# A scaled copy at the DMA's pace: five token tiles cut to 26, 25, 26, 25, 26, and the later weights loaded as 16 rows a tile and dealt out by TensorE

## The chip, the core and the metric

The kernel runs on one core of a Trainium2 chip. The metric is the device time of one launch in microseconds; the shorter the better. Beside the time of each run there is a profile of one execution, whose span counts from the first to the last recorded instruction. TensorE, VectorE (DVE), ScalarE (ACT) and GpSimd (POOL) each run their own stream of instructions; SyncE (SP) issues most of the DMA transfers, and sixteen DMA engines carry them.

## The reference

The kernel is the dispatch half of a mixture of experts, without the routing: every token's row is written out once for each of its two experts, scaled by that expert's weight. The indices of the experts are not used.

```python
batch, seq, hidden, n_experts = 16, 1024, 512, 8
k = 2
# x: (16, 1024, 512) f32, expert_weights: (16, 1024, 2) f32
x_expanded = x[:, :, np.newaxis, :].repeat(k, axis=2)
weights = expert_weights[..., np.newaxis]
return (x_expanded * weights).astype(np.float32)
```

So 33.6 MB of x and 131 KB of weights are read, and 67.1 MB are written, with one multiplication for each number written.

## The kernel before

The 16,384 tokens are spread over 128 partitions, 128 tokens to a partition. "Token" below means one such slot: 128 tokens at once, one in each partition, 2 KB of x and 4 KB of output in each. They are cut into five tiles (`groups`), 25, 25, 25, 25 and 28 tokens. Within a tile a partition's tokens lie together in memory, so a load or a store is one long contiguous piece for each partition.

Three buffers fill most of the on-chip memory: `x_pair`, two buffers for x, one for the even tiles and one for the odd ones; `o_ring`, one output buffer of 25 tokens (`TX`); and `w_tile`, all weights, two for each token in each partition. The output buffer is worked in two halves, tokens 0 to 12 (`CUT` = 13) and the rest. In each half VectorE multiplies the first 8 tokens (9 in the first tile) in operations of four tokens (`vector`, through `product`, L97), and ScalarE the others, one expert's row at a time (`scalar`, L120). Then the half is stored.

All transfers but one go through `move` (L65), which issues them from SP in the order in which the program names them. SP is one queue: an issue that waits holds all behind it. The one other transfer, the first tile's weights, is issued by ScalarE. SP's order is:

- the first tile's x in two loads, 9 and 16 tokens (`STEPS`), then all of tile 1's x;
- when the products of tile 0 have been made, tile 2's x, 21 and then 4 tokens, into the buffer that tile 0 leaves, and the weights of tiles 1 to 4, one transfer each (`weights`, L85), 50 or 56 floats to each of 128 partitions;
- tile 0's two stores. The first is held (`wait`, L69) until the load of 21 tokens has landed, so that a stretch of reading from memory ends before a stretch of writing begins;
- tile 1's two stores, then tile 3's x, then tile 4's x in 24 and 4 tokens, and behind it tile 2's two stores, again held until the larger of the two loads has landed;
- tile 3's two stores and tile 4's two stores of 13 and 12 tokens;
- the last tile has 28 tokens and the output buffer 25, so its last three are multiplied into the front of the buffer once the store of that half has landed, and go out as a third piece (L159 to L162).

Of the kernel before, what the change touches and what calls it, by code (L numbers as in the profile page):

```python
# [1 line left out]

# [4 lines left out]


@with_exitstack
def kernel(  # L10
    ctx: ExitStack,
    tc: tile.TileContext,
    x: bass.AP,
    expert_indices: bass.AP,
    expert_weights: bass.AP,
    out: bass.AP,
):
    nc = tc.nc

    batch, seq, hidden = x.shape  # L20
    k = expert_weights.shape[-1]
    P = nc.NUM_PARTITIONS
    ntok = batch * seq
    assert ntok % P == 0
    A_TOTAL = ntok // P

    f32 = mybir.dt.float32
    row = k * hidden
    CH = 4


    groups = [25, 25, 25, 25, 28]
    TX = 25
    CUT = 13
    STEPS = {0: [9, 16], 2: [21, 4], 4: [24, 4]}
    assert sum(groups) == A_TOTAL

    xf = x.rearrange("b s h -> (b s) h")
    of = out.rearrange("b s k h -> (b s) (k h)")
    wf = expert_weights.rearrange("b s k -> (b s) k")  # L40

    w_pool = ctx.enter_context(tc.tile_pool(name="w_pool", bufs=1))
    x_pool = ctx.enter_context(tc.tile_pool(name="x_pool", bufs=1))
    o_pool = ctx.enter_context(tc.tile_pool(name="o_pool", bufs=1))

    w_tile = w_pool.tile([P, A_TOTAL * k], f32)
    o_ring = o_pool.tile([P, TX * row], f32)
    x_pair = [
        x_pool.tile([P, max(groups[e::2]) * hidden], f32, name=f"x{e}")
        for e in range(2)  # L50
    ]

    def rows(of_all, done, T):
        return of_all[done * P : (done + T) * P, :].rearrange(
            "(p a) n -> p (a n)", a=T
        )

    tiles = []
    done = 0
    for n in groups:  # L60
        tiles.append((done, n))
        done += n


    def move(out, in_):  # L65
        return tc.keep_in_program_order(nc.sync.dma_start(out=out, in_=in_))  # L66


    def wait(ins, done):  # L69
        tc.add_manual_dep(  # L70
            ins.ins,
            done.ins.name,
            mybir.DependencyInfo(
                mybir.DependencyClass.Sync, mybir.DependencyReason.DATA
            ),
            reason="turn",
        )

    def load(i, e):
        at = sum(STEPS.get(i, groups[i : i + 1])[:e])  # L80
        to = at + STEPS.get(i, groups[i : i + 1])[e]
        part = slice(at * hidden, to * hidden)
        return move(x_pair[i % 2][:, part], rows(xf, *tiles[i])[:, part])

    def weights(g, to):  # L85
        at, n = tiles[g]
        w = w_tile[:, at * k : (at + (to - g) * n) * k]
        return (
            w.rearrange("p (g m) -> p g m", g=to - g),
            wf[at * P : (at + (to - g) * n) * P, :].rearrange(  # L90
                "(g p a) n -> p g (a n)", g=to - g, p=P
            ),
        )

    def product(o_tile, t, x_in, c, m):
        o = t * row
        nc.vector.tensor_tensor(  # L97
            out=o_tile[:, o : o + m * row].rearrange(
                "p (t k h) -> p t k h", t=m, k=k
            ),  # L100
            in0=x_in[:, : m * hidden]
            .rearrange("p (t h) -> p t h", t=m)
            .unsqueeze(2)
            .to_broadcast([P, m, k, hidden]),
            in1=w_tile[:, c : c + m * k]
            .rearrange("p (t k) -> p t k", t=m)
            .unsqueeze(3)
            .to_broadcast([P, m, k, hidden]),
            op=mybir.AluOpType.mult,
        )  # L110


    def vector(src, c, at, to):
        for t in range(at, to, CH):
            u = min(t + CH, to)
            product(o_ring, t, src[:, t * hidden : u * hidden], c + t * k, u - t)

    def scalar(src, c, at, to):
        return [
            nc.scalar.mul(  # L120
                out=o_ring[:, e * hidden : (e + 1) * hidden],
                in_=src[:, e // k * hidden : (e // k + 1) * hidden],
                mul=w_tile[:, c + e : c + e + 1],
            )
            for e in range(at * k, to * k)
        ]

    def store(dst, at, to):
        return move(dst[:, at * row : to * row], o_ring[:, at * row : to * row])


    out_w, in_w = weights(0, 1)
    nc.scalar.dma_start(out=out_w, in_=in_w)
    load(0, 0)
    load(0, 1)
    load(1, 0)
    for i, (done, n) in enumerate(tiles):
        src, dst, c = x_pair[i % 2], rows(of, done, n), done * k
        v = 9 if i == 0 else 8
        held = i in (0, 2)  # L140
        for at, to in [(0, CUT), (CUT, TX)]:
            vector(src, c, at, at + v)
            scalar(src, c, at + v, to)
            if not held:
                store(dst, at, to)
        if held:
            if i == 0:
                last = load(2, 0)
                load(2, 1)
                for g in range(1, len(tiles)):  # L150
                    move(*weights(g, g + 1))
            else:
                last = load(4, 0)
                load(4, 1)
            for at, to in [(0, CUT), (CUT, TX)]:
                wait(store(dst, at, to), last)
        elif i == 1:
            load(3, 0)
        if n > TX:  # L159
            m = n - TX  # L160
            product(o_ring, 0, src[:, TX * hidden :], c + TX * k, m)
            move(dst[:, TX * row :], o_ring[:, : m * row])  # L162

# [1 line left out]
_INS = ['x', 'expert_indices', 'expert_weights']  # L165
_OUTS = [((16, 1024, 2, 512), 'float32')]


# [23 lines left out]
```

## Time and profile before

| | |
|---|---|
| median of 3 runs | 238.79 us (238.78 to 238.80) |
| the profiled execution | 238.92 us |
| its span | 237.1 us |
| VectorE, ScalarE, GpSimd busy | 93.1, 54.9, 0.2 us |
| SP's DMA queue, share of sixteen engines' span | 98.7% |
| read and written | 33.69 and 67.11 MB |

The page of the profile gives busy times for each engine, the span in forty slices (a digit is tenths, 9 is 90% or more), the DMA queues with the time their packets took, a chain of waits followed back from the last instruction, and groups of instructions by line with their mean duration and with what ended the idle time before them. The timeline lists instructions by start and length in microseconds; for a DMA the issuing instruction stands there, and the time to its landing in the list of issues. TensorE does no work in this kernel.

### The profile page before, as it was taken

The page shows a single profiled execution, that of the slowest core. Times are in us where ns is not written, and L with a number is a line of the kernel's source. Part 1 is how long each engine was busy: PE and PEld are TensorE (multiplying, and loading weights), DVE is VectorE, ACT ScalarE, POOL GpSimd, SP SyncE. Part 2 cuts the span into 40 slices and gives each one's busy share as a digit, 9 for nine tenths or more (in the row PEclk, how much of TensorE's full clock was granted, in tenths as well). Part 3 has the DMA queues.
Part 4 walks back from the last instruction along what each step waited for, and adds up shares of the span by engine and source line. Part 5 has one row for each costly group of instructions (what it writes and reads, how often), then busy time and mean ns, then how long its engine had stood idle before and what let it go on. Part 6 is the DMA issues. An engine that isn't in the chain of part 4 may idle for free.

```text
span 237.1 us, 217 instructions
## 1 busy us (share of the span) xinstructions
DVE 93.1 (39%) x23; ACT 54.9 (23%) x87; POOL 0.2 (0%) x4
## 2 busy tenths in 40 slices
DVE  0499800000094580954900000039195292861300
ACT  0008800000090520914400000037080270800000
POOL 0000000000000000000000000000000000000000
DMA  7999989899999999999999999999999999999996
GB/s 260 474 445 475 423 370 464 372 486 431 420 398 497 464 431 420 398 398 409 475 478 406 398 453 431 431 409 457 484 431 431 409 398 434 449 449 456 423 398 265
DMA packets 3457, 100.80 MB, mean 425 GB/s; under 512 B 1024, under 2 KB 1024, under 8 KB 1024
## 3 DMA queue, kind: packets, MB, share of 16 engines
q1 hardware_dynamic: 3312, 100.77, 98.7%
q10 hardware_dynamic: 144, 0.03, 0.1%
q14 instruction: 1, 0.01, 0.0%
HBM read 33.69 MB, written 67.11 MB: 425 GB/s over the span
## 4 chain that ended last, share of the span: by engine, by line
DMA 70%; DVE 16%; ACT 4%; issue 3%; SPq 0%; DVEq 0%; ACTq 0%
DMA out_dram<-o_ring 46%; DMA x<-in_x_dram 24%; DVE o_ring L97 16%; ACT o_ring L120 3%; ACT L120 1%; SPq L66 0%; DVEq L97 0%; ACTq L120 0%
## 5 line engine op out<-in xcount | busy, mean ns | idle before, releaser
L97 DVE TENSOR_TENSOR o_ring<-x,w_tile 128x4096 f32<-128x4096 f32 (+2 forms) x23 | 93.1, 4096 | 128.5 <-DMA out_dram<-o_ring 105.6
L120 ACT ACTIVATE o_ring<-x,w_tile 128x512 f32<-128x512 f32 x86 | 53.7, 709 | 134.0 <-DMA out_dram<-o_ring 123.3
L120 ACT ACT_TABLE_LOAD x1 | 1.3, 1283 | 18.6 <-DMA x<-in_x_dram 18.6
L176 POOL MEMSET const-bfloat16-1.0<- 128x1 bf16 x1 | 0.1, 102 | 0.0
L176 POOL MEMSET const-uint8-127<- 128x1 uint8 x1 | 0.1, 102 | 0.0
L176 POOL MEMSET const-float32-0.0<- 128x1 f32 x1 | 0.1, 99 | 0.2 <-issue 0.2
L176 POOL MEMSET const-float32-1.0<- 128x1 f32 x1 | 0.1, 99 | 0.0
## 6 DMA issues: line engine op xcount, KB each, us to landing
out_dram<-o_ring SPq DMA_DIRECT2D x5, 6656.0 KB, 21.3
out_dram<-o_ring SPq DMA_DIRECT2D x5, 6144.0 KB, 21.6
x<-in_x_dram SPq DMA_DIRECT2D x2, 6400.0 KB, 34.1
x<-in_x_dram SPq DMA_DIRECT2D x1, 6144.0 KB, 20.6
x<-in_x_dram SPq DMA_DIRECT2D x1, 5376.0 KB, 18.8
x<-in_x_dram SPq DMA_DIRECT2D x1, 4096.0 KB, 17.4
x<-in_x_dram SPq DMA_DIRECT2D x1, 2304.0 KB, 8.1
x<-in_x_dram SPq DMA_DIRECT2D x2, 1024.0 KB, 21.4
```

Of the source, the lines that this page charges most:

```text
L97: nc.vector.tensor_tensor(out=o_tile[:, o : o + m * row].rearrange("p (t k h) -> p t k h", t=m, k=k), in0=x_in[:, : m * hidden] .rearrange ...
L120: nc.scalar.mul(out=o_ring[:, e * hidden : (e + 1) * hidden], in_=src[:, e // k * hidden : (e // k + 1) * hidden], mul=w_tile[:, c + e : c ...
L176: nc = _bacc.Bacc("TRN2", target_bir_lowering=False, num_devices=1)
```

## The change

The tiles become 26, 25, 26, 25 and 26 tokens, and the output buffer 26. Every tile is then stored in two pieces, 13 and 13 or 13 and 12, and the code for the third piece goes. The loads in two steps become 9 and 17, 21 and 5, 22 and 4.

The weights of tiles 1 to 4 are no longer loaded into `w_tile` from behind tile 2's x. They are loaded between the two loads of the first tile, each as 16 rows of 8 x 50 or 8 x 52 floats into 16 partitions, into the part of `o_ring` that the second half of tile 0 will fill later (`room`). Such a row holds what belongs to eight neighbouring partitions. `deal` spreads it: GpSimd makes an identity matrix in `room`; for each tile TensorE transposes eight blocks of 16 rows into a tile in PSUM, ScalarE copies that to `room` with the order of the columns changed, TensorE transposes it back as a whole into one PSUM tile for all four, and ScalarE copies this to `w_tile`. `deal` stands in the program behind the products of the first half of tile 0; in the built program ScalarE's five copies stand ahead of all its multiplications, and the first operation of VectorE's second half waits for the rows, TensorE and GpSimd.

```diff
-    groups = [25, 25, 25, 25, 28]
-    TX = 25
+    groups = [26, 25, 26, 25, 26]
+    TX = max(groups)
     CUT = 13
-    STEPS = {0: [9, 16], 2: [21, 4], 4: [24, 4]}
+    STEPS = {0: [9, 17], 2: [21, 5], 4: [22, 4]}
...
-    def weights(g, to):
...
+    R = 16
+    Q = P // R
+    room = o_ring[:, CUT * row :]
+    eye = room[:, :P]
+    dealt = tiles[1:]
+    skip = dealt[0][0] * k
+    raw = [
+        room[:R, P + (at * k - skip) * Q : P + ((at + n) * k - skip) * Q]
+        for at, n in dealt
+    ]
+    turned = room[:, P + (A_TOTAL * k - skip) * Q :]
+
+    def deal():
+        nc.gpsimd.memset(eye, 1.0)
+        nc.gpsimd.affine_select(
+            out=eye,
+            in_=eye,
+            pattern=[[-1, P]],
+            compare_op=mybir.AluOpType.is_equal,
+            fill=0.0,
+            base=0,
+            channel_multiplier=1,
+        )
+        back = ps_pool.tile([P, A_TOTAL * k - skip], f32)
+        for g, (at, n) in enumerate(dealt):
+            m = n * k
+            mid = ps_pool.tile([m, P], f32, name=f"mid{g}")
+            flat = turned[:m, g * P : (g + 1) * P]
+            for q in range(Q):
+                nc.tensor.transpose(
+                    mid[:, q * R : (q + 1) * R],
+                    raw[g][:, q * m : (q + 1) * m],
+                    eye[:R, :R],
+                )
+            nc.scalar.copy(
+                out=flat.rearrange("m (r q) -> m q r", q=Q),
+                in_=mid.rearrange("m (q r) -> m q r", q=Q),
+            )
+            c = at * k - skip
+            nc.tensor.transpose(back[:, c : c + m], flat, eye[:m, :m])
+        nc.scalar.copy(out=w_tile[:, skip:], in_=back)
...
-    out_w, in_w = weights(0, 1)
-    nc.scalar.dma_start(out=out_w, in_=in_w)
+    nc.scalar.dma_start(out=w_tile[:, :skip], in_=rows(wf, *tiles[0]))
     load(0, 0)
+    for to, (at, n) in zip(raw, dealt):
+        move(
+            to,
+            wf[at * P : (at + n) * P, :].rearrange("(r m) n -> r (m n)", r=R),
+        )
     load(0, 1)
     load(1, 0)
...
-        for at, to in [(0, CUT), (CUT, TX)]:
+        for at, to in [(0, CUT), (CUT, n)]:
             vector(src, c, at, at + v)
             scalar(src, c, at + v, to)
+            if i == 0 and at == 0:
+                deal()
...
                 last = load(2, 0)
                 load(2, 1)
-                for g in range(1, len(tiles)):
-                    move(*weights(g, g + 1))
...
-        if n > TX:
-            m = n - TX
-            product(o_ring, 0, src[:, TX * hidden :], c + TX * k, m)
-            move(dst[:, TX * row :], o_ring[:, : m * row])
```

More of the change, by code (lines that the diff above doesn't have):

```diff
@@ L83, in load @@
         return move(x_pair[i % 2][:, part], rows(xf, *tiles[i])[:, part])
-    def weights(g, to):
[L86 to L92, printed above, removed]
-        )
+    R = 16
[19 more added lines that the diff above has]
+            channel_multiplier=1,
+        )
+        back = ps_pool.tile([P, A_TOTAL * k - skip], f32)
[16 more added lines that the diff above has]
+        nc.scalar.copy(out=w_tile[:, skip:], in_=back)
     def product(o_tile, t, x_in, c, m):
@@ L154 @@
                 load(4, 1)
-            for at, to in [(0, CUT), (CUT, TX)]:
+            for at, to in [(0, CUT), (CUT, n)]:
                 wait(store(dst, at, to), last)
```

2 lines of the change are left out of this document (added).

## The prediction

> **What bounds the kernel now.** I read the page first (engines, the forty slices, the queues), then the chain of waits, then the timeline for the starts of single pieces. The page:
>
> ```profile
> span 237.1 us, 217 instructions
> DVE 93.1 (39%) x23; ACT 54.9 (23%) x87; POOL 0.2 (0%) x4
> ...
> DMA  7999989899999999999999999999999999999996
> ...
> q1 hardware_dynamic: 3312, 100.77, 98.7%
> q10 hardware_dynamic: 144, 0.03, 0.1%
> q14 instruction: 1, 0.01, 0.0%
> HBM read 33.69 MB, written 67.11 MB: 425 GB/s over the span
> ```
>
> VectorE works 39% of the span and ScalarE 23%, while SP's queue q1 fills 98.7% of what the sixteen DMA engines have: 234.0 of 237.1 us. Only the first and last slices fall to 7 and 6 tenths. So the end moves only if q1 gets more or less to do, or if it runs dry somewhere. The bytes of x and of the output are fixed, and both kernels move them once.
>
> The pace comes from the timeline of VectorE in the last third. Each of these starts follows the landing of one stored piece:
>
> ```profile
> 157.85 8.76 DVE L97 TENSOR_TENSOR o_ring<-x,w_tile 128x4096 f32<-128x4096 f32 x2 [39.07 <-DMA out_dram<-o_ring]
> 172.39 8.76 DVE L97 TENSOR_TENSOR o_ring<-x,w_tile 128x4096 f32<-128x4096 f32 x2 [5.77 <-DMA out_dram<-o_ring]
> 188.08 8.76 DVE L97 TENSOR_TENSOR o_ring<-x,w_tile 128x4096 f32<-128x4096 f32 x2 [6.93 <-issue]
> 202.57 8.76 DVE L97 TENSOR_TENSOR o_ring<-x,w_tile 128x4096 f32<-128x4096 f32 x2 [5.73 <-DMA out_dram<-o_ring]
> 218.29 3.36 DVE L97 TENSOR_TENSOR o_ring<-x,w_tile 128x3072 f32<-128x3072 f32 x1 [6.97 <-DMA out_dram<-o_ring]
> ```
>
> From 157.85 to 218.29 are 60.44 us, in which pieces of 12, 13, 12 and 13 tokens landed: 50 tokens of 128 x 4096 B, 26.21 MB, so 433.7 GB/s, or 1.209 us for a stored token and 0.604 us for a loaded one. At this pace the 100.77 MB of q1 take 232.4 us; the 4.7 us left of the span are the start, the end and small items. That is the whole room there is.
>
> The chain of waits shows where q1 might run dry. Its columns are start, length and what:
>
> ```profile
> 1.16 17.37 DMA x<-in_x_dram
> ...
> 27.64 18.75 DMA x<-in_x_dram
> 46.39 0.02 issue
> 46.41 18.56 DMA out_dram<-o_ring
> ...
> 139.52 18.14 DMA out_dram<-o_ring
> ...
> 188.08 8.77 DVE o_ring L97 x2
> 196.85 0.02 SPq L66
> 196.87 0.03 issue
> 196.90 21.27 DMA out_dram<-o_ring
> ```
>
> At 139.52 the first store of tile 2 is issued behind the 4 tokens of the second load of tile 4. It lands 18.14 us later, and 4 loaded plus 13 stored tokens at the pace above are 2.42 + 15.72 = 18.13 us. So 2.42 us of queued work are enough to cover the time from an issue to its first bytes: nothing is lost there. I use 2.42 us below as a cover that suffices.
>
> **The change part by part.**
>
> *The four weight transfers leave the middle.* At 46.41 the first store of tile 0 is issued behind the same 4 loaded tokens and also the four weight transfers, and takes 18.56 us for the same 13 tokens. So the four cost 18.56 - 18.14 = 0.42 us of q1. Their bytes, 204 floats for each of 128 partitions, 104,448 B, are 0.24 us at the pace above; the rest is the price of small pieces. Removed: -0.42 us.
>
> ```profile
> 29.16 1.90 SPq L66 DMA_DIRECT2D w_tile<-in_expert_weights_dram  x4
> ...
> w_tile<-in_expert_weights_dram SPq DMA_DIRECT2D x3, 25.0 KB, 19.7
> w_tile<-in_expert_weights_dram SPq DMA_DIRECT2D x1, 28.0 KB, 19.1
> ```
>
> They had also served as cover for the store at 46.41. Without them 2.42 us would be left; with the fifth token that moves from the first to the second load of tile 2 it is 5 x 0.604 = 3.02 us. Both are at or above the 2.42 us that suffice: 0.
>
> *The same bytes come back between the first tile's two loads*, as four transfers of 16 rows of 1,600 or 1,664 B. Sixteen long pieces in place of 128 short ones speak for less than 0.42 us; that all of them are written into 16 partitions speaks for more. No row of this trace shows such a transfer. Below: their bytes at the full pace, 0.24 us, and not less unless the start hides them (the first slice is at 7 tenths), then 0. Above: if the pace follows the number of partitions written, 16 of 128, it is 54.2 GB/s and 1.93 us. The nearest row is that of the same four transfers with nearly the same bytes, so I take their 0.42 us, and keep 0 and 1.93 as ends. Their issue takes SP 1.90 us by the row above, now ahead of the second load, which would go out near 3.0 us in place of 1.1. It is covered by the first load:
>
> ```profile
> 9.01 19.70 DVE L97 TENSOR_TENSOR o_ring<-x,w_tile 128x4096 f32<-128x4096 f32 x6 [9.01 <-DMA w_tile<-in_expert_weights_dram]
> 18.60 1.28 ACT L120 ACT_TABLE_LOAD   x1 [18.60 <-DMA x<-in_x_dram]
> 19.90 8.68 ACT L120 ACTIVATE o_ring<-x,w_tile 128x512 f32<-128x512 f32 x14
> ```
>
> ```profile
> L97 DVE TENSOR_TENSOR o_ring<-x,w_tile 128x4096 f32<-128x4096 f32 x20 | 87.6, 4421 | 121.5 <-DMA out_dram<-o_ring 98.7 <-issue 13.9 <-DMA w_tile<-in_expert_weights_dram 9.0
> L97 DVE TENSOR_TENSOR o_ring<-x,w_tile 128x1024 f32<-128x1024 f32 x2 | 2.4, 1217 | 0.0
> ```
>
> VectorE starts at 9.01, when the first nine tokens and the weights of tile 0 are there, so q1 is busy nearly until then: 0. The two groups below it are VectorE's operations of four tokens and of one.
>
> [...]
>
> *The first tile's order.* Its second load carries 17 tokens in place of 16. It lands at 18.53 now (1.16 + 17.37), then at 18.53 + 0.60 + 0.42 = 19.55. VectorE has its first nine tokens done at about 19.1 (two operations of 4.42 us and one of 1.22 from 9.01), so it waits some 0.4 us for the second half. The first load of tile 2 needs two operations more and goes out at 19.55 + 8.84 = 28.4 in place of 27.64. q1 then still holds the rest of tile 1: its 25 tokens end 25 x 0.604 = 15.1 us after 19.55, at 34.7. That leaves 6.3 us of cover where 2.42 suffice: 0, with 3.9 us to spare.
>
> *Dealing out.* TensorE makes 32 small transposes and 4 wide ones, ScalarE four copies of 50 or 52 partitions x 128 and one of 128 x 204, GpSimd a memset and a select on 128 x 128. The rows land near 9.5 us. ScalarE's five copies stand ahead of its multiplications, which wait for the second load anyway; its table load moves into the same idle stretch. VectorE's second half writes over the scratch, so it waits for the last transpose. All this has from 9.5 to 19.55, 10 us, and then 3.9 us until q1 runs dry. Five copies at the price of the 128x512 multiplication, 709 ns, are 3.5 us:
>
> ```profile
> L120 ACT ACTIVATE o_ring<-x,w_tile 128x512 f32<-128x512 f32 x86 | 53.7, 709 | 134.0 <-DMA out_dram<-o_ring 123.3
> L176 POOL MEMSET const-uint8-127<- 128x1 uint8 x1 | 0.1, 102 | 0.0
> ```
>
> The transposes have no row; (13.9 - 3.5) / 36 leaves 0.29 us for each, hand-offs included, before anything is late. GpSimd's part is unpriced too, but can start 8 us before the rows are there. I take 0. What is late next, if this cover goes, is the first load of tile 2.
>
> *Tiles of 26 and 25; the third piece goes.* The same 128 tokens are stored; the tightest compute cover stays that of the last tile, whose first store is issued at 196.90, while the piece ahead lands at 202.57: 5.7 us, and 12-token pieces ahead of it remain. In 26-token tiles ScalarE gets ten multiplications in each half, 7.1 us at 709 ns, under VectorE's 8.77: 0. What ends is the third transfer of the last tile:
>
> ```profile
> 221.68 0.33 SPq L66 DMA_DIRECT2D out_dram<-o_ring  x1
> ...
> out_dram<-o_ring SPq DMA_DIRECT2D x1, 1536.0 KB, 14.7
> ```
>
> It lands at 221.68 + 14.7 = 236.4. From the landing before 218.29, about 218.2, to there are 18.2 us, and 15 tokens are 18.13 us. So one transfer more costs 0 to 0.1 us beside its bytes; its 3.36 us of VectorE are hidden behind the 12 tokens queued. I take -0.05 us.
>
> *Instruction fetch.* The one q14 packet of 0.01 MB was fetched on one DMA engine. TensorE's new instructions may add one or two; 8 KB on one of sixteen engines at 27.1 GB/s are 0.3 us, felt only if that engine ends last. I take 0 and keep +0.3.
>
> Sum: -0.42 + 0.42 - 0.05 = -0.05 us on the profiled execution's 238.92 us (its span of 237.1 and 1.8 around it), so 238.87. The median of the runs, 238.79, lies 0.13 us under it; from the median the forecast is 238.74, given as 238.7. A time within 0.2% (0.48 us) is what a measurement of this kernel can hardly tell from no change; the forecast lies well inside.
>
> **The rivals.**
>
> *A, slower: the sixteen partitions.* All engines write into the same few partitions at once, and the four transfers hold q1 up right behind the first nine tokens. It decides from 0.95 us for the four (0.95 - 0.42 - 0.05 = +0.48): 239.3; at the upper end, 1.93 us, it is +1.46 and 240.2. [...] Against it: the amount is small, and the DMA's start is not full, so part of the delay may fall where engines idle.
>
> *B, faster: the rows cost nothing at the start.* Then -0.42 - 0.1 = -0.52 us, 238.3, just past 0.2%. For it: 16 long pieces, and the first slice at 7 tenths. Against it: the second slice, in which the rows move, is already at 9 tenths, so the bytes still take 0.24 us, and then it is -0.28 and 238.5, not faster by 0.2%.
>
> *C, slower: the dealing out ends too late.* VectorE's second half waits for the scratch beyond 23.5 us (19.55 + 3.9), and every microsecond beyond is one on the end, since q1 runs dry before the first load of tile 2. At 0.5 us each, 36 transposes take 18 us, and with the copies 21.5 from 9.5: 31, so 7.5 us late and 246. Against it: they are tiles of 16 and 128 columns, while ScalarE handles 128x512 in 0.7.
>
> **How the numbers follow.** The forecast, the four transfers between 0.24 and 0.95 us, has 0.74; its own range is 238.5 to 239.2. A has 0.16, B 0.07, C 0.03. So faster 0.07, same 0.74, slower 0.19. The range from 238.3 takes in B, and up to 239.5 the milder part of A, with an added fetch; what it leaves out is C and the far part of A, about 0.1, and a little of B.
>
> **What would show it.** In the profile after, q1 should again fill 98 to 99% and the span be 236.8 to 237.4. The landing of the second load tells the price of the rows: 19.4 to 19.6 as forecast, 20.1 or later with A, 19.1 with B. The last transpose should end before 19.5, and VectorE's second half follow the load and not TensorE; the other way round is C. The first load of tile 2 should be issued near 28.4, and the store held for its landing should land 15.72 + 3.02 = 18.7 us after its issue; more is a cover that was too short. A last landing under 0.7 us before the span's end, as now, is a tail that did not change. The prediction is wrong if q1 has a gap anywhere or the rows cost over 0.95 us.

## The result, and the profile after

The changed kernel is slower: 240.12 us (median of 6 runs, 239.60 to 240.49) beside 238.78 us (238.74 to 238.80) for the kernel before, ratio 1.0056 with a 95% interval of 1.0044 to 1.0067. A second time, in another set of runs, it took 239.88 us beside 238.97 us, ratio 1.0039 (1.0024 to 1.0054). The forecast was 238.7 us in a range from 238.3 to 239.5.

The first six runs lie in two groups, three at 239.6 to 239.8 and three at 240.4 to 240.5. The profiled execution is of the lower group, 239.82 us with a span of 238.1, so it explains 0.90 us of the loss (238.92 before), not 1.34.

The page of the changed kernel:

```profile
span 238.1 us, 305 instructions
...
DMA  7999999899999999999999899999999999999996
...
q1 hardware_dynamic: 2720, 100.77, 98.6%
q10 hardware_dynamic: 144, 0.03, 0.1%
q14 instruction: 1, 0.01, 0.0%
HBM read 33.69 MB, written 67.11 MB: 423 GB/s over the span
```

q1 moves the same 100.77 MB in 2,720 packets where there were 3,312, and is still full: 98.6% of 238.1 are 234.8 us, where 98.7% of 237.1 were 234.0. So the queue did not run dry. The same bytes took longer.

Where, the chain of waits tells (start, length, what):

```profile
3.40 17.07 DMA x<-in_x_dram
...
29.42 18.90 DMA x<-in_x_dram
...
141.75 18.19 DMA out_dram<-o_ring
```

The second load of the first tile lands at 3.40 + 17.07 = 20.47 us. Before it was 18.53, and the forecast, with one token more and 0.42 us for the rows, was 19.55. So 0.92 us too much are there after 20 of 238 us. The later steps move by that: the first load of tile 2 goes out at 29.42 and not at 28.4. The store held at 141.75 lands 18.19 us after its issue where it was 18.14, so that cover held.

The timeline of the changed kernel, first for the dealing out and then for the starts of VectorE that follow a landed store:

```profile
13.13 0.34 PE L130 MATMUL back<-o_ring 52*128 52x52 f32 x1 [0.20 <-ACT o_ring L125]
13.51 0.33 ACT L131 COPY w_tile<-back 128x204 f32<-128x204 f32 x1 [0.43 <-PE back L130]
20.59 9.90 DVE L135 TENSOR_TENSOR o_ring<-x,w_tile 128x4096 f32<-128x4096 f32 x3 [0.68 <-DMA x<-in_x_dram]
67.36 8.76 DVE L135 TENSOR_TENSOR o_ring<-x,w_tile 128x4096 f32<-128x4096 f32 x2 [36.87 <-DMA out_dram<-o_ring]
...
98.63 8.76 DVE L135 TENSOR_TENSOR o_ring<-x,w_tile 128x4096 f32<-128x4096 f32 x2 [6.95 <-DMA out_dram<-o_ring]
...
160.01 8.76 DVE L135 TENSOR_TENSOR o_ring<-x,w_tile 128x4096 f32<-128x4096 f32 x2 [38.10 <-DMA out_dram<-o_ring]
...
205.90 8.76 DVE L135 TENSOR_TENSOR o_ring<-x,w_tile 128x4096 f32<-128x4096 f32 x2 [5.76 <-DMA out_dram<-o_ring]
```

The weights are dealt out at 13.51 + 0.33 = 13.8 us, 6.6 us before the second load lands, and VectorE's second half waits for that load (0.68 us), not for TensorE. The kernel before had the same starts at these places:

```profile
65.05 8.76 DVE L97 TENSOR_TENSOR o_ring<-x,w_tile 128x4096 f32<-128x4096 f32 x2 [36.34 <-DMA out_dram<-o_ring]
...
95.24 8.76 DVE L97 TENSOR_TENSOR o_ring<-x,w_tile 128x4096 f32<-128x4096 f32 x2 [6.93 <-issue]
```

Put against the plan of the prediction (a loaded token 0.60, a stored one 1.21 us, and the weights the same 0.42 us early as late), the delay at each step is as follows. The first row is a landing by the chain of waits; the next four are starts of VectorE, which lie 0.08 to 0.19 us behind the landing of the store itself.

| step | after - before | plan | over the plan |
|---|---|---|---|
| second load | 20.47 - 18.53 = 1.94 | 1.02 | 0.92 |
| tile 0, first store | 67.36 - 65.05 = 2.31 | 1.21 | 1.10 |
| tile 1, first store | 98.63 - 95.24 = 3.39 | 2.42 | 0.97 |
| tile 2, first store | 160.01 - 157.85 = 2.16 | 1.21 | 0.95 |
| tile 3, second store | 205.90 - 202.57 = 3.33 | 2.42 | 0.91 |
| profiled time | 239.82 - 238.92 = 0.90 | -0.05 | 0.95 |

Nearly all of the loss of this execution is there at the end of the second load, and the later steps stay within 0.2 us of it.

### The profile page after: what moved, and what is told of

It is laid out like the page before. It is cut to its first block, busy times and chain, and to the rows that moved or that the text cites. A ratio compares the mean times of both kernels' runs of the same rounds, so it can differ in the third digit from the quotient of the medians.

```text
span 238.1 us, 305 instructions
## 1 busy us (share of the span) xinstructions
PE 3.0 (1%) x36; PEld 2.4 (1%) x36; DVE 89.9 (38%) x22; ACT 60.4 (25%) x98; POOL 0.7 (0%) x6
## 3 DMA queue, kind: packets, MB, share of 16 engines
q1 hardware_dynamic: 2720, 100.77, 98.6%
## 4 chain that ended last, share of the span: by engine, by line
DMA 70%; DVE 17%; DVEq 2%; SPq 1%; issue 0%
DMA out_dram<-o_ring 46%; DMA x<-in_x_dram 23%; DVE o_ring L135 17%; DVEq L225 2%; SPq L70 1%; DVEq L135 0%
## 5 line engine op out<-in xcount | busy, mean ns | idle before, releaser
L135 DVE TENSOR_TENSOR o_ring<-x,w_tile 128x4096 f32<-128x4096 f32 (+1 forms) x22 | 89.9, 4131 | 124.8 <-DMA out_dram<-o_ring 107.2
L158 ACT ACTIVATE o_ring<-x,w_tile 128x512 f32<-128x512 f32 x92 | 57.3, 708 | 139.7 <-DMA out_dram<-o_ring 123.6
L125 ACT COPY o_ring<-mid 50x128 f32<-50x128 f32 (+1 forms) x4 | 1.5, 386 | 9.1 <-PE mid L120 9.1
L120 PE MATMUL mid<-o_ring 16*50 16x16 f32 (+1 forms) x32 | 1.9, 201 | 10.3 <-DMA o_ring<-in_expert_weights_dram 10.3
L120 PEld LDWEIGHTS mid<-o_ring 16*50 16x50 f32 (+1 forms) x32 | 1.6, 132 | 10.5 <-issue 10.3
L130 PE MATMUL back<-o_ring 50*128 50x50 f32 (+1 forms) x4 | 1.4, 344 | 0.2 <-ACT o_ring L125 0.2
L130 PEld LDWEIGHTS back<-o_ring 50*128 50x128 f32 (+1 forms) x4 | 0.7, 179 | 0.5 <-ACT o_ring L125 0.4
## 6 DMA issues: line engine op xcount, KB each, us to landing
x<-in_x_dram SPq DMA_DIRECT2D x1, 5376.0 KB, 18.9
```

The source lines that it names most:

```text
L120: nc.tensor.transpose(mid[:, q * R : (q + 1) * R], raw[g][:, q * m : (q + 1) * m], eye[:R, :R],)
L125: nc.scalar.copy(out=flat.rearrange("m (r q) -> m q r", q=Q), in_=mid.rearrange("m (q r) -> m q r", q=Q),)
L130: nc.tensor.transpose(back[:, c : c + m], flat, eye[:m, :m])
L135: nc.vector.tensor_tensor(out=o_tile[:, o : o + m * row].rearrange("p (t k h) -> p t k h", t=m, k=k), in0=x_in[:, : m * hidden] .rearrange ...
L158: nc.scalar.mul(out=o_ring[:, e * hidden : (e + 1) * hidden], in_=src[:, e // k * hidden : (e // k + 1) * hidden], mul=w_tile[:, c + e : c ...
```

## The experiments

Sixteen kernels ran in four rounds, e1 to e4, e5 to e8, e9 to e12 and e13 to e16; the kernels of a round share the runs of the kernel before, and each round ran on another chip. Each has one profile. "Second load" is its landing by the chain of waits or, where the chain does not pass it (e5, e12), ScalarE's first start less the 0.07 us that lay between the two before.

| run | kernel | second load | median, us | before, us | ratio (95%) |
|---|---|---|---|---|---|
| e1 | rows, not dealt out | 20.22 | 239.92 | 238.99 | 1.0037 (1.0022-1.0052) |
| e2 | old form, early | 19.95 | 239.39 | 238.99 | 1.0016 (1.0007-1.0026) |
| e3 | no later weights | 19.43 | 239.69 | 238.99 | 1.0027 (1.0015-1.0039) |
| e4 | new tiles alone | 19.40 | 239.41 | 238.99 | 1.0019 (1.0009-1.0028) |
| e5 | before, again | 18.63 | 239.06 | 238.97 | 1.0003 (0.9993-1.0013) |
| e6 | changed, again | 20.88 | 239.88 | 238.97 | 1.0039 (1.0024-1.0054) |
| e7 | new tiles alone, again | 19.43 | 239.44 | 238.97 | 1.0024 (1.0013-1.0034) |
| e8 | rows, spread out | 19.99 | 239.38 | 238.97 | 1.0023 (1.0014-1.0033) |
| e9 | rows of 8 | 21.03 | 240.35 | 239.05 | 1.0056 (1.0041-1.0070) |
| e10 | before, rotated | 18.68 | 239.08 | 239.05 | 1.0006 (0.9997-1.0014) |
| e11 | new tiles alone, third time | 19.37 | 239.41 | 239.05 | 1.0018 (1.0009-1.0026) |
| e12 | before, weights on ScalarE's queue | 18.75 | 239.26 | 239.05 | 1.0013 (1.0005-1.0021) |
| e13 | new tiles, first in two blocks | 19.50 | 239.33 | 238.91 | 1.0017 (1.0008-1.0026) |
| e14 | new tiles, third piece | 19.29 | 239.27 | 238.91 | 1.0020 (1.0011-1.0029) |
| e15 | new tiles, rotated | 19.40 | 239.23 | 238.91 | 1.0015 (1.0007-1.0024) |
| e16 | before, three engines late | 19.61 | 239.73 | 238.91 | 1.0037 (1.0024-1.0049) |

### First round: the place, the shape, the dealing out, the tiles

My first theory was the place: small transfers between two loads leave the next load's first packets to wait out their reading. In the trace's packet records, one entry for each piece that a DMA engine moves, the first packets of the second load took 1.65 to 2.06 us in the changed kernel where the later ones took 1.29. The rivals were the shape of the rows and the dealing out; the tiles were taken for free.

e1 leaves `deal()` out and fills the later weights with a constant:

```diff
+    nc.gpsimd.memset(w_tile[:, skip:], 1.0)
     load(0, 0)
...
-            if i == 0 and at == 0:
-                deal()
```

> The changed kernel with the four row transfers where they are, but without the dealing out: no TensorE work, no copies, the weights of tiles 1 to 4 are the constant 1 and not the loaded ones. Theory PLACE (small transfers between the first two loads leave the first packets of the next load with their whole read time to wait) and theory SHAPE (sixteen pieces written into the same 16 partitions block the queue) both expect the changed kernel's own time, 239.6 to 240.5 us, and the second load landing near 20.5 us. Theory DEALING (something of the transposes and copies costs the time) expects 238.7 and a landing near 19.5.

e2 keeps the new tiles and moves the old form of the transfers to the early place:

```diff
     load(0, 0)
+    for g in range(1, len(tiles)):
+        move(*weights(g, g + 1))
     load(0, 1)
...
-                for g in range(1, len(tiles)):
-                    move(*weights(g, g + 1))
```

> New tiles; the later weights are loaded in the old form, 128 pieces of 200 or 208 B a tile straight to their place, but between the first tile's two loads; no dealing out. PLACE: about as slow as the changed kernel, 239.6 to 240.5 us, since the loads are broken at the same place. SHAPE: as the kernel before, 238.7 to 238.9, the second load landing at 19.5 us (0.42 us for the transfers).

e3 is e2 without those transfers, the later weights set to 1:

```diff
-    for g in range(1, len(tiles)):
-        move(*weights(g, g + 1))
+    nc.gpsimd.memset(w_tile[:, tiles[1][0] * k :], 1.0)
```

> New tiles, the weights of tiles 1 to 4 not loaded at all (they are the constant 1). Both theories: the floor, 238.79 - 0.42 - 0.05 = 238.3 us, the second load landing at 18.53 + 0.60 = 19.1 us. If it is slower than 238.6, the new tile sizes cost something that the sum left out.

e4 is the kernel before with the new `groups`, `TX` and `STEPS` and without the third piece.

> The new tile sizes and nothing else: the later weights in the old form and at the old place, behind tile 2's x. Both theories: 238.79 - 0.05 = 238.7 us. Slower than 239.2 would put part of the loss on the tiles.

The second loads in the four, by their chains of waits, e1, e2, e3 and e4 in this order:

```profile
3.25 16.97 DMA x<-in_x_dram
```

```profile
3.33 16.62 DMA x<-in_x_dram
```

```profile
1.17 18.26 DMA x<-in_x_dram
```

```profile
1.17 18.23 DMA x<-in_x_dram
```

So the load lands at 20.22 with the rows, 19.95 with the old form, 19.43 without either and 19.40 with the weights at the old place. The dealing out is cleared: e1 is 0.93 us slower than the kernel before, the changed kernel of the next round (e6) 0.91. The place is cleared of most: the old form there costs 19.95 - 19.40 = 0.55 us of the load and nothing of the time beside e4. The rows cost 0.82 us of the load, 0.27 us more than the old form at the same place, and by the medians 0.53 us of the time over it; the intervals of the two ratios still overlap (from 1.0022 and up to 1.0026). What no theory of mine had expected is e4: the new tiles alone cost 0.42 us. And e3, with less to move than e4, is not faster but 0.28 us slower, inside the scatter of the two (239.36 to 239.83 and 239.10 to 239.84). So taking 0.42 us of work away from the queue need not show at the end.

The semaphore records tell where e3 lost its lead. They have sixteen entries for a wide transfer (before's first load has them from 8.27 to 8.81 us). I take each for the landing of one DMA engine's share; the records do not name the engine. When the first store lands, e3's last engine is 0.65 to 0.80 us ahead of e7's and e4's (66.11 us beside 66.76 and 66.91). When tile 3's load lands, it is level with them (128.09 beside 128.18 and 128.10).

### Second round: the same chip for all, and the rows spread out

e5, e6 and e7 are the kernel before, the changed one and the new tiles alone, once more, for profiles that can be set side by side. e8 is e1 with the rows sent to 16 partitions that lie apart:

```diff
-        room[:R, P + (at * k - skip) * Q : P + ((at + n) * k - skip) * Q]
+        room[: 7 * R : 7, P + (at * k - skip) * Q : P + ((at + n) * k - skip) * Q]
```

> The kernel before, unchanged, profiled on the same chip as the next three. The first four runs have made a new theory, TILES: the new tile sizes alone cost 0.4 us, as wider gaps between the first and the last of the sixteen DMA engines from the first load on, and 0.2 to 0.4 us where the stores of tile 1 meet the load of tile 3. If so, this profile shows the first load landing within 0.55 us of its first engine (8.3 to 8.8), as the first profile of before did. If that spread and the meeting belong to the chip and not to the tiles, it shows 0.8 us or more here too, and the ratio is 1.000 either way.

> The changed kernel, unchanged, beside the others of this call. TILES plus ROWS (0.5 us more for the rows than for the old form at the same place, from the first packets of the second load, 1.9 us in place of 1.3): about 1.0 us over before, ratio 1.004. If dealing out costs something beside that, it is slower than the rows without dealing, which had 1.0037.

> The new tile sizes alone, a second time, on this chip. TILES: 0.3 to 0.5 us over before again, ratio 1.0013 to 1.0020. If the first time was the chip's noise: 1.0000, 0.05 us under before.

> As the rows without dealing out, but each transfer's 16 rows go to partitions 0, 7, 14 to 105 in place of 0 to 15 (weights of tiles 1 to 4 constant). SHAPE in the sense of the same few partitions written by all engines: the first packets of the second load fall from 1.9 back to 1.3 us, the second load lands at 19.4 to 19.6 us and the time is that of the tiles alone. PIECES (16 long pieces, one on each engine, with a semaphore behind each, whatever the partitions): no change, 1.9 us and a landing at 20.2 to 20.5.

The second load of the changed kernel (e6) and of the spread rows (e8):

```profile
3.31 17.57 DMA x<-in_x_dram
```

```profile
3.98 16.01 DMA x<-in_x_dram
```

The partner of e8 is e1 of the first round, the same kernel but for the partitions; e6 also deals out. From e1 to e8 the second load's landing falls from 20.22 to 19.99 us and the median from 239.92 to 239.38, that of the tiles alone (239.44). The ratios, 1.0037 and 1.0023, have intervals that overlap (from 1.0022 and up to 1.0033). The first packets of the next load took more than its later ones by 0.64 us an engine in all in e1, 0.69 in e6 and 0.38 in e8, while the pieces of the rows themselves, four to an engine, took 70 to 76 ns on average in e1, 85 to 93 in e6 and 68 to 70 in e8, so 0.27 to 0.37 us for four. So more of the price falls on what stands behind the rows than on the rows, and spreading the partitions takes off less than half of that. The first packets at 1.65 us and the landing at 19.99 lie between what the two theories expected, 1.3 and 1.9 us, 19.4 to 19.6 and 20.2 to 20.5. At both places sixteen long pieces cost the packets behind them something (0.64 and 0.38 us); behind the old form's 128 short ones (e2) the first packets took 1.3 us, no more than the later ones.

Over the tiles alone the rows cost the second load 0.82 us in e1 (20.22 - 19.40), 1.07 in the profile after (20.47 - 19.40) and 1.45 in e6 (20.88 - 19.43). The 0.6 us that e8 still pays (19.99 - 19.40) show that the neighbouring partitions are not the whole price.

The tiles are confirmed as a second loss. VectorE's starts in e5:

```profile
18.70 1.28 ACT L120 ACT_TABLE_LOAD   x1 [18.70 <-DMA x<-in_x_dram]
65.18 8.76 DVE L97 TENSOR_TENSOR o_ring<-x,w_tile 128x4096 f32<-128x4096 f32 x2 [36.39 <-DMA out_dram<-o_ring]
...
95.33 8.76 DVE L97 TENSOR_TENSOR o_ring<-x,w_tile 128x4096 f32<-128x4096 f32 x2 [6.90 <-issue]
...
157.84 8.76 DVE L97 TENSOR_TENSOR o_ring<-x,w_tile 128x4096 f32<-128x4096 f32 x2 [38.96 <-DMA out_dram<-o_ring]
...
202.56 8.76 DVE L97 TENSOR_TENSOR o_ring<-x,w_tile 128x4096 f32<-128x4096 f32 x2 [5.80 <-DMA out_dram<-o_ring]
```

And in e7, the new tiles alone:

```profile
19.50 1.28 ACT L120 ACT_TABLE_LOAD   x1 [19.50 <-DMA x<-in_x_dram]
66.84 8.76 DVE L97 TENSOR_TENSOR o_ring<-x,w_tile 128x4096 f32<-128x4096 f32 x2 [37.50 <-DMA out_dram<-o_ring]
...
98.25 8.76 DVE L97 TENSOR_TENSOR o_ring<-x,w_tile 128x4096 f32<-128x4096 f32 x2 [6.94 <-issue]
...
159.90 8.76 DVE L97 TENSOR_TENSOR o_ring<-x,w_tile 128x4096 f32<-128x4096 f32 x2 [38.33 <-DMA out_dram<-o_ring]
...
205.64 8.76 DVE L97 TENSOR_TENSOR o_ring<-x,w_tile 128x4096 f32<-128x4096 f32 x2 [5.73 <-DMA out_dram<-o_ring]
```

Over the plan (0.60, 1.21, 2.42, 1.21, 2.42 us) the tiles are late by 0.20 us at the second load, 0.45 at the first store, 0.50 at tile 1's, 0.85 at tile 2's and 0.66 at tile 3's second. So here too half or more is there by 67 us, for the engine that lands last. The mean of the sixteen engines tells another place: it is 0.09 us behind the plan in e7 when tile 1's first store lands, and 0.35 us behind when tile 3's load has landed (e4: 0.05 and 0.26). A possible cause showed in the semaphore records: the first load lands on the sixteen DMA engines over 0.59 us in e5 (0.54 in the first profile of before), over 0.93 in e7 (0.84 in e4), and over 2.07 in e6 (1.37 in the first profile of the changed kernel). A wide transfer's 128 pieces have sixteen landings, and if every engine has its own share of each, an engine that starts late could stay late.

### Third round: half the partitions, other addresses, the other queue

e9 is e1 with `R = 8`: rows twice as long into half as many partitions.

> As the rows without dealing out, but each tile's weights as 8 rows of twice the length, into partitions 0 to 7 (weights of tiles 1 to 4 constant; same bytes, same four transfers). SHAPE (all pieces crowd into a few partitions and what follows waits behind them): half the partitions, about twice the price; the second load lands some 1 us later than with 16 rows (about 21 in place of 20), and the time is about 0.5 to 1 us over that of the rows without dealing, ratio 1.006 to 1.008. PIECES (few long pieces with a semaphore each): as with 16 rows or less, ratio 1.004.

```profile
2.69 18.34 DMA x<-in_x_dram
```

The load lands at 21.03, 1.63 us over the 19.40 of the tiles alone, twice the 0.82 of e1, as the theory of the shape expected. The time, 1.0056, is the slowest of the sixteen kernels but less than expected, and its interval is clear of those of the spread rows and of the old form. One thing beside the partitions differs: each transfer has eight pieces, and by its landings only eight engines carry it, so twice the bytes for each of them are a rival that this run does not part from the partitions.

e10 gives the last tile of 28 the first rows of memory, so that all other tiles begin 28 tokens further on:

```diff
-    done = 0
-    for n in groups:
+    done = groups[-1]
+    for n in groups[:-1]:
         tiles.append((done, n))
         done += n
+    tiles.append((0, groups[-1]))
```

> The kernel before with its old tiles, but the last tile of 28 takes the first rows of x and of the output, so every other tile begins 28 tokens further in memory. Sizes and order of all transfers are the same. ADDRESSES (where the tiles begin decides what the meeting of tile 1's stores with tile 3's load costs): the time moves by 0.1 us or more against before. SIZES (pieces of 26 and 13 tokens): 1.0000.

e11's label says rotated, but the kernel that ran under it is the new tiles alone, not rotated, as its expectation has it; the rotated one is e15.

> The new tile sizes alone, a third time, as the partner of the next kernel on this chip: ratio 1.0019 and 1.0024 before, so 0.4 to 0.5 us over before.

e12 leaves the old tiles and issues the later weights from ScalarE at the start:

```diff
+    for g in range(1, len(tiles)):
+        out_g, in_g = weights(g, g + 1)
+        nc.scalar.dma_start(out=out_g, in_=in_g)
     load(0, 0)
...
-                for g in range(1, len(tiles)):
-                    move(*weights(g, g + 1))
```

> The old tiles; the later weights in the old form, 128 pieces of 200 or 224 B, but all issued by ScalarE at the start, on its own queue beside the first loads, and no longer by SP. If a second queue fills gaps that the first load's start leaves, up to the 0.42 us of the four transfers is gained: 238.4 us, ratio 0.998. If the DMA engines only share themselves out, it is moved and not gained: ratio 1.000, and the second load lands 0.3 to 0.5 us later than the 18.5 us of before.

The addresses do nothing that can be told from 1: the ratio is 1.0006 (0.9997 to 1.0014). The tiles cost 0.36 us a third time. The other queue does not gain: the kernel is 0.21 us slower. By the semaphore records the four transfers land between 18.9 and 49.6 us, one behind each load, and they are paid there one by one: against e5 the last engine is 0.11 us late at the second load, 0.21 at tile 1's x and 0.36 at tile 2's first load. At tile 0's first store, where e5 has paid for its own transfers, 0.11 us are left. The loss comes later: 0.09 us behind when tile 1's first store lands, 0.75 when tile 3's load lands.

### Fourth round: what of the tiles it is

e13 lays the first tile out as two blocks of 13 tokens:

```diff
...
+                    last = move(
+                        x_pair[0][:, a * hidden : z * hidden],
+                        rows(xf, CUT * e, CUT)[:, (a - CUT * e) * hidden : (z - CUT * e) * hidden],
+                    )
...
```

> The new tile sizes alone, but the first tile of 26 is laid out in memory as two blocks of 13 tokens, so the first load steps 26,624 B from partition to partition in place of 53,248 (old tiles: 51,200); one load and one small weight transfer more, about 0.1 us. PITCH (the first load's step through memory makes the DMA engines start further apart, and that spread, 0.8 to 0.95 us from the first to the last engine in place of 0.5 to 0.7, costs at the meetings of loads and stores and at the end): spread back to 0.6 us, ratio 1.000 to 1.001. If it is not the first tile's layout: 1.0018 to 1.0024 as before, or more.

e14 stores the last tile as 13, 10 and 3 tokens:

```diff
+        if i == 4:
+            cuts = [(0, CUT), (CUT, 23), (23, n)]
...
```

> The new tile sizes alone, but the last tile goes out in three pieces, 13, 10 and 3 tokens, as the old last tile did. If the third piece was worth having (the end of the kernel is gentler on the engines): ratio down to 1.000. By the stages of the profiles, where the loss is there before the last tile begins: unchanged, 1.0020, or 0.05 us more.

e15 makes e10's change in the new tiles.

> The new tile sizes, with the last tile taking the first rows of memory, so every other tile begins 26 tokens further on. ADDRESSES of the tiles: another time than the new tiles alone by 0.1 us or more. SIZES: the same, 1.0018 to 1.0024.

None of the three undoes the loss: 1.0017, 1.0020, 1.0015. The third piece is not it, nor where the tiles begin in memory. The load steps (`STEPS`) and the size of the output buffer (`TX`), which change with the tiles, were not tried apart. e13 is not decisive: its first load landed over 0.76 us, between the two kinds of tiles, and it has 0.1 us more to do.

e16 leaves the old tiles and makes three of the sixteen engines late, with one small transfer into three partitions:

```diff
     load(0, 0)
+    move(o_ring[:3, 20 * row : 20 * row + 3072], xf[:18, :].rearrange("(r a) n -> r (a n)", r=3))
     load(0, 1)
```

> The kernel before, old tiles, with one transfer more between the first tile's two loads: 3 rows of 12,288 B on 3 of the 16 DMA engines, read into a part of the output buffer that is overwritten later. It makes three engines 0.46 us late and leaves the others alone. SPREAD (engines far apart cost at the meetings of loads and stores and at the end): about as slow as the new tiles, 0.3 to 0.5 us, ratio 1.0013 to 1.0020, if the three are not the earliest. If a late engine is no cost beyond its own lateness and is partly hidden: 0 to 0.2 us.

```profile
19.69 1.28 ACT L120 ACT_TABLE_LOAD   x1 [19.69 <-DMA x<-in_x_dram]
66.08 8.76 DVE L97 TENSOR_TENSOR o_ring<-x,w_tile 128x4096 f32<-128x4096 f32 x2 [36.54 <-DMA out_dram<-o_ring]
...
158.76 8.76 DVE L97 TENSOR_TENSOR o_ring<-x,w_tile 128x4096 f32<-128x4096 f32 x2 [39.27 <-DMA out_dram<-o_ring]
...
203.35 8.76 DVE L97 TENSOR_TENSOR o_ring<-x,w_tile 128x4096 f32<-128x4096 f32 x2 [5.71 <-DMA out_dram<-o_ring]
```

36 KB more, 0.085 us of the queue, put the second load 0.99 us later than in e5 (19.69 against 18.70), the first store 0.90, tile 2's 0.92, tile 3's second 0.79, and the median is 0.82 us over the kernel before. Three engines are late, not all sixteen: by the semaphore records thirteen land the second load at 18.30 to 18.65 us, where e5's sixteen land at 18.02 to 18.63, and three at 19.05, 19.43 and 19.62.

They are late alone as far as tile 1's first store: when it lands the median engine is 0.30 us behind e5's and the last one 0.90. When tile 3's load lands, at 125.86 us, the median engine is 0.75 us behind and the last 0.96, and the sixteen landings lie within 0.79 us (0.58 in e5). So in e16 the lateness that three engines get in the first 20 us, 0.99 us, is paid at the end almost in full, 0.82 us in the median, though thirteen engines had nothing more to do; and it is paid because the thirteen lose their lead between 96 and 126 us, not because three end alone. That is shown, in one profile. What takes it from them is not.

That stretch, from the landing of tile 1's first store to that of tile 3's load, moves 12 stored and 25 loaded tokens in every kernel. It takes the mean of the sixteen engines 29.70 to 29.75 us in the three profiles with old tiles and no transfer added or moved (before, e5, e10), and 29.79 to 30.15 us in the fifteen others. So some of the loss, little in e13 to e15 (29.79 to 29.80) and most in e3 and e16 (30.15 and 30.10), is made where all kernels move the same. The queue does not run dry there: in the pages of before, after, e5 and e16 every slice from 95 to 130 us is at nine tenths or more. It is the last pieces of tile 1's second store that take longer: its pieces take 1.815 us in the median of every profile, but the last sixteen to start take 2.31 us on average in e16, 2.26 in e3, 2.08 in e7 and 1.90 in e5. In e16 the first of the sixteen to start takes 2.87 us and the last 1.82, so it is the engines ahead that are slowed. What slows them was not tried.

That the new tiles lose their 0.4 us through late engines is not shown. In the five profiles with old tiles the first load lands over 0.47 to 0.71 us, in the six with new tiles and no early rows or weights over 0.68 to 0.94, so they mostly start wider; but e14, with the narrowest of these (0.68), lost as much as the others, and nothing that I changed in the tiles took the loss away.

## Why the prediction was wrong

- What bounds the kernel: right. q1 is full in both, 98.7 and 98.6%.
- The rows, taken at 0.42 us from the row of the old transfers with "nearly the same bytes": wrong. This is one of the two steps that failed, at the second load much the larger one and in the medians about as large as the other. The nearest row in bytes was not the nearest in shape. Over the tiles alone the second load lands later by 1.07 us in the profile after, 0.82 in e1 and 1.45 in e6. In the medians the rows are 0.53 us over the old form (e1, e2), 0.50 over the spread rows (e6, e8) and 0.44 over the tiles alone (e6, e7). That lies between my two ends, 0 and 1.93, and is rival A, with its sign and its mark (20.1 or later; 20.47 came, with some 0.2 us of the tiles in it). The prediction's own sign of being wrong, rows over 0.95 us, came in the profile after and in e6, not in e1. A had 0.16.
- "Tiles of 26 and 25" at 0 and the third piece at -0.05: wrong, and no rival had it. Five kernels with these tiles and the weights in the old form at the old place were 0.32 to 0.47 us slower than before, every interval clear of 1. Of my two terms the third piece is cleared (e14); the failure is the 0 for the tiles.
- Beneath both lies one assumption of the sum: it took q1 as one server at 433.7 GB/s. In the profile after the second load lands sixteen times, from 19.62 to 20.47 us, and VectorE starts behind the last of them, at 20.59; bytes over pace met the mean of the sixteen where the two were compared (15.71 us beside 15.72, below). e16 shows the difference: 0.085 us of bytes, 0.82 us of time.
- Removing the transfers from the middle, -0.42: the price was right where it stood. From the landing of tile 2's second load to that of tile 0's first store the mean engine takes 15.71 us in the profile after, the pace's 15.72 for 13 tokens, and 16.12 in e7. At the end it was not seen: e3, without the transfers at any place, is no faster than e4 with them, within the scatter.
- The dealing out at 0: right. It ends at 13.8 us, and 239.88 with it stands beside 239.92 without. 36 transposes and five copies took from 10.3 to 13.8 us.
- The covers: right where the forecast gave a number. The first held store, behind 5 tokens, was issued at 48.34 and landed at 67.17, 18.83 us beside 18.7; the second, behind 4 tokens, took 18.19 beside 18.13.
- The instruction fetch at 0: right, one packet on q14 as before. From the last landing to the end of the span are 0.89 us, and before they were 0.81, not under 0.7 as I had read it: the tail is much the same.
- One more reading was off and moved nothing: the four transfers of the kernel before carry 206 floats a partition, not 204, which are 0.24 us all the same.
- Rival B, the rows hidden in the start, fell: no kernel with rows was faster.

What stays open: why the tiles of 26 and 25 lose 0.3 to 0.5 us; why so many kernels lose time between tile 1's first store and tile 3's load; and the upper group of the first six runs, 240.4 to 240.5 us, of which there is no profile.

## What to carry to other kernels

When a DMA queue is full from end to end, as q1 is here at 98.4 to 98.8%, count per DMA engine and not only bytes over the whole: in e16 0.085 us of bytes made three engines late early on and cost 0.82 us at the end. Here a small transfer was not priced by its bytes alone: the same 104 KB delayed the second load by 0.55 us as short pieces to 128 partitions (e2), by 0.6 as sixteen rows that lie apart (e8), by 0.8 to 1.45 as sixteen neighbouring rows (e1, after, e6) and by 1.6 as eight (e9). And price a new access by the row nearest in shape; where the trace has none, the sum has an open end and the forecast should lean there.

## What the runs showed that I had not expected

- One transfer of three rows of 12,288 B cost 0.82 us of 239, ten times its share of the queue.
- The old form, 512 pieces of 200 or 208 B, was the cheapest at the early place, 0.55 us of the second load (e2) beside 0.6 to 1.6 for rows, though it has eight times as many packets as the rows.
- The new tiles scatter more: 239.1 to 240.3 us over ten runs in e7, where the kernel before lay within 238.8 to 239.2 in 25 runs of the same round.
